# A hybrid retention, mLSTM and feed-forward layer: context keys and values of all heads made first, transposes and scan steps placed later

## The chip, the core and the metric

The kernel runs on one core of a Trainium2 chip. Its engines are TensorE (PE, matrix products; PEld is its weight load), VectorE (DVE), ScalarE (ACT), GpSimd (POOL) and SyncE (SP), whose queue issues nearly all DMA transfers. The metric is the time of one execution on the chip in microseconds (us); the time before is the median of three runs.

## The reference

One layer over 1024 latent tokens of width 1024, with 256 context tokens ahead of them. Two token mixers share one input projection: retention with 4 heads of 128, and mLSTM with 4 heads of 128. Each scans in chunks of 128 tokens in both directions, over the context first, and the latent scan starts from the context's final state. Cut to what matters:

```python
hc = modulate(rms_norm(ctx, norm1_gain), csh1, csc1)      # 256 context tokens
feats_c, post_c = mixer_inputs(hc, w_in, ..., None)       # no rotation
ret_c, ml_c, st_f, st_b = bidirectional_scans(feats_c, log_gamma, zero, zero)
hx = modulate(rms_norm(x, norm1_gain), sh1, sc1)          # 1024 latent tokens
feats_x, post_x = mixer_inputs(hx, w_in, ..., rope)       # q and k of the retention heads rotated
ret_x, ml_x, _, _ = bidirectional_scans(feats_x, log_gamma, st_f, st_b)
x = x + g1 * mixer_output(ret_x, ml_x, *post_x, w_ret_up, w_ml_up, w_out)
x = x + g2 * swiglu(modulate(rms_norm(x, norm2_gain), sh2, sc2), w_ffn_in, w_ffn_out)
return rms_norm(x, final_gain)                            # the context itself is not returned
```

Shift, scale and gate (`sh1`, `sc1`, ...) come from a product of SiLU(c) with the adaLN weights. Of the context only keys, values and mLSTM gates matter, since its outputs are not returned.

## The kernel before

Every fp32 operand of a large product is split into two parts, high and low, and a product is three matmuls: high by high, high by low, low by high. `split` makes the high part on ScalarE (L182) and the low part on VectorE (L183). A weight tile of 128x512 is loaded into `raw` (four buffers) by SP's queue and split into `fw` (eight buffers).

**Start.** The eight tiles of the first half of x are loaded, then the adaLN weights (32 tiles, L396). The context comes later (`load_ctx`), as do the weights of head 0. x and the context are normalized and modulated tile by tile (`scaled_tile`), and head 0's products on the first half of x run between the adaLN products (`first_tiles`, L428 to L430). Head 0 takes its products plainly.

**Heads 1 to 7.** A head has two blocks: one for k and v, one for q and the output gate. A block is a Winograd product of seven products of twelve matmuls of 512 columns (`winograd_block`, `prod`, L251), with left factors that `Factors` makes of four weight tiles and right factors (`t1` to `t4`) that are made once, on VectorE, after head 0. `run_blocks` interleaves the last two products of a block with the first of the next, and after each product calls `tick`, by which the work "beside" advances: the mLSTM gates beside head 1, and from head 2 on the scan of head u - 2, each with a rate in steps per tick:

```python
                if u >= 2:
                    beside(scan(u - 2), 1.3)
```

**Context.** In the k and v block of every head, after its fifth product, `context_kv` computes keys and values of the 256 context tokens: 48 matmuls of 256 columns (L559 to L561) with the head's weights as the stationary operand, four transposes (L568), and a store to `kv_d`. The split context was stored to DRAM (`ctx_d`) and is loaded again for each head in four pairs of tiles (`context_stream`); the right weights need one more factor, `a21`, in these blocks.

**Outputs of a block.** `head_done` gets each quarter. A retention head's k and q are rotated (`rotated`): two DMAs swap the halves, GpSimd and VectorE combine them (L521 to L524). `store_tokens` transposes k, v and the mLSTM gate on TensorE (L509), four transposes a quarter, and stores them.

**Scan.** One step a slot, with each part of a chunk's work in a slot of its own. `load` and `load_qk` bring k, v and q of a chunk (`qk` has two buffers), `decay` scales v on GpSimd (L806), `advance` updates the state (L820), `stage_a` scales q, `stage_b` makes the scores (L866), `stage_c` the output (L883 to L885), `norm_y` normalizes four chunks on VectorE (L910), and `put_y` transposes them (L915):

```python
        for j in range(8):
            after(5 + j, load_qk, j)
            at(6 + j, stage_a, j)
            at(7 + j, stage_b, j)
            at(8 + j, stage_c, j)
        for j0 in (0, 4):
            at(12 + j0, norm_y, j0)
            at(13 + j0, put_y, j0)
```

After the heads come eight blocks for the merge gates (scans 6 and 7 beside the first of them), the up and output projections, the feed-forward part and its output.

The order of instructions on each engine is not the order in which the code writes them: the framework's scheduler places each instruction on its engine, and each engine then works its list in order, waiting where an operand or a buffer is not ready.

Of the kernel before, what the change touches and what calls it, by code (L numbers as in the profile page):

```python
# [17 lines left out]
P = 128  # L18
# [3 lines left out]
KT = 8  # L22
# [12 lines left out]
def body(tc, a, out):  # L35
# [173 lines left out]
    class Factors:  # L209
# [3 lines left out]
        def __init__(self, src, a21=False):  # L213
            self.src, self.a21, self.made = src, a21, []
# [4 lines left out]
        def make(self, r):  # L219
# [13 lines left out]
            if self.a21:  # L233
                yield parts_of(r["a21"])

        def need(self, n=8):
# [32 lines left out]
    def winograd_block(w, x, t, done, new, snaps, tail=None):  # L269
# [35 lines left out]
        if tail is not None:  # L305
            tail()
# [38 lines left out]
    def wt(dt=F32):  # L345
        return pw.tile([P, 512], dt, tag="wt", bufs=5, name=nm("wt"))
# [16 lines left out]
    ctx_d = dram.tile([2, 4, P, 512], F32, name="ctx_d")  # L363
# [9 lines left out]
    def ssq_of(xr, n):  # L373
        ss = [st.tile([P, 512], F32, tag="ss", bufs=2, name=nm("ss"))[:, :n] for _ in range(2)]
        for kt in range(KT):
# [3 lines left out]
            else:  # L379
                sq = st.tile([P, 512], F32, tag="sq", bufs=2, name=nm("sq"))[:, :n]  # L380
# [33 lines left out]
    def plain_pair(w, src, kh):  # L414
        for f in range(2):
            raw = w_raw()
            nc.sync.dma_start(raw, src[kh, f])
            w[("a11", "a21", "a12", "a22")[2 * kh + f]] = parts_of(raw)

    first_ps = [mm_ps(), mm_ps()]  # L420

    def first_tiles(kts):

        for f in range(2):
            for kt in kts:
                wh, wl = (t[:, kt % 4 * P:(kt % 4 + 1) * P] for t in w_kv[("a11", "a21", "a12", "a22")[2 * (kt // 4) + f]])
                hi, lo = xh[0][0][:, kt, :], xh[0][1][:, kt, :]
                nc.tensor.matmul(first_ps[f], lhsT=wh, rhs=hi, start=kt == 0, stop=False, skip_group_check=True)  # L428
                nc.tensor.matmul(first_ps[f], lhsT=wh, rhs=lo, start=False, stop=False, skip_group_check=True)
                nc.tensor.matmul(first_ps[f], lhsT=wl, rhs=hi, start=False, stop=kt == KT - 1, skip_group_check=True)  # L430

    load_x(x_raw[0], a["xT"][0])
# [14 lines left out]

    def scaled_x(hf, kt):
# [3 lines left out]
        (0, 3): lambda: cols_of("x0", x_raw[0], 512),  # L452
        (2, 5): lambda: cols_of("c", c_raw, CTX),
        (3, 5): lambda: cols_of("x1", x_raw[1], 512),
    }
    loads = {
        9: lambda: plain_pair(w_kv, a["win"][0], 0),
        14: lambda: plain_pair(w_kv, a["win"][0], 1),
        19: load_ctx,
        25: lambda: load_x(x_raw[1], a["xT"][1]),  # L460
        36: lambda: plain_pair(w_qg, a["win"][1], 0),
        38: lambda: plain_pair(w_qg, a["win"][1], 1),
    }
    for cb in range(4):
        ada_ps[cb] = sc_ps()[:2, :]
        for kt in range(KT):
# [27 lines left out]
    kv_d = [dram.tile([P, NCH, 2, P], F32, name=f"kv_d{u}") for u in range(2 * H)]  # L494
# [10 lines left out]
    def store_tokens(c, dst):  # L505

        pt_ = sc_ps()
# [6 lines left out]
    def head_done(u, part):  # L514
        def rotated(c, hf, scale):
# [4 lines left out]
            o = wt()  # L520
# [9 lines left out]
        def done(f, hf, c):  # L530
            n0 = slice(2 + 4 * hf, 6 + 4 * hf)
            t = slice(hf * 512, hf * 512 + 512)
            if part == 0 and f == 0:
                o = rotated(c, hf, None) if u < H else c
                nc.sync.dma_start(qk_d[u][:, 1, t], o)
                store_tokens(o, kv_d[u][:, n0, 0, :])
            elif part == 0:
                store_tokens(c, kv_d[u][:, n0, 1, :])
# [8 lines left out]
            else:  # L547
                store_tokens(c, g_d[u][:, 4 * hf:4 * hf + 4, :])
        return done

    def context_kv(u, w, parts):

        pk, pv = sc_ps(), sc_ps()
        for kt in range(KT):
            hi, lo = parts(kt)
            for f, ps in enumerate((pk, pv)):
                wh, wl = (t[:, kt % 4 * P:(kt % 4 + 1) * P] for t in w(2 * (kt // 4) + f))
                o = ps[:, :CTX]
                nc.tensor.matmul(o, lhsT=wh, rhs=hi, start=kt == 0, stop=False)  # L559
                nc.tensor.matmul(o, lhsT=wh, rhs=lo, start=False, stop=False)  # L560
                nc.tensor.matmul(o, lhsT=wl, rhs=hi, start=False, stop=kt == KT - 1)  # L561
        c = wt()
        nc.scalar.copy(c[:, :CTX], pk[:, :CTX])
        nc.scalar.copy(c[:, CTX:], pv[:, :CTX])
        pt_ = sc_ps()
        for n in range(2):
            for f in range(2):
                nc.tensor.transpose(pt_[:, (2 * n + f) * P:(2 * n + f + 1) * P], c[:, f * CTX + n * P:f * CTX + (n + 1) * P], ident)  # L568
        o = wt()
        nc.scalar.copy(o, pt_)  # L570
        nc.sync.dma_start(kv_d[u][:, 0:2], o.rearrange("p (n f c) -> p n f c", n=2, f=2))

    def context_stream():

        last = {}

        def parts(kt):
            if kt % 2 == 0:
                for i in range(2):
                    last[i] = wt(F32R)  # L580
                    nc.sync.dma_start(last[i].bitcast(F32), ctx_d[i, kt // 2])
# [811 lines left out]
```

## Time and profile before

| | us |
|---|---|
| median of three runs (lowest, highest) | 1719.94 (1718.01, 1721.85) |
| the profiled execution | 1724.97 |
| its span in the trace | 1723.2 |
| TensorE busy | 1607.6 (93%) |
| VectorE busy | 1008.2 (59%) |
| ScalarE busy | 690.9 (40%) |
| GpSimd busy | 434.2 (25%) |

The stages in the span: start and head 0 to 126.7 us, head 1 to 211.9, heads 2 to 7 to 656.1, the first merge gates with the last scans to 770, the other gates and projections to 1075, the feed-forward products to 1460, their output to the end. In a row of a table by stage stand the stretch, its length, and then the busy time of PE, PEld, DVE, ACT and POOL with the number of instructions; behind them the granted clock of TensorE as a share of full speed, the share of the DMA engines, and GB/s. A wait stands with the instruction that waited, what released it, the total, the count and the longest.

### The profile page before, as it was taken

To read this page: it belongs to the slowest core of one execution; us is meant where nothing else is said; L and a number is where in the kernel's file an instruction comes from. 1 tells how busy PE (TensorE), PEld (TensorE's weight loads), DVE (VectorE), ACT (ScalarE), POOL (GpSimd) and SP (SyncE) were. 2 spreads that over 40 slices of the span, in tenths; PEclk is the share of its full clock that TensorE was granted. 3 is DMA by queue.
4 is the path that set the end of the run, shared out by engine and by line. 5 is a ranking of instruction groups with operands and counts; after the bars stand their busy time and mean duration, and the time that the engine had idled before them with its cause. 6 is when DMAs were issued, how large, how long until landed. Compare 5 with 4: busy or idle time off the path is not lost.

```text
span 1723.2 us, 23184 instructions
## 1 busy us (share of the span) xinstructions
PE 1607.6 (93%) x7702; PEld 1300.6 (75%) x7702; DVE 1008.2 (59%) x1986; ACT 690.9 (40%) x1355; POOL 434.2 (25%) x504
## 2 busy tenths in 40 slices
PE   7987788888998989999999999999999999999997
PEld 2665667777777777878888887788888888888887
DVE  4568757575575757766444579555554454636343
ACT  4433333333343436665422345334444334524230
POOL 1251134343233434421022026322222221000001
PEclk9998889999999999999999999999999999999998
DMA  9433376676767766645645440432222223845531
GB/s 319 151 107 103 111 241 209 215 232 196 235 202 220 225 203 192 193 128 176 216 139 185 157 142 6 134 93 85 90 88 80 74 85 118 276 120 154 195 92 50
DMA packets 188632, 268.64 MB, mean 156 GB/s; under 512 B 19504, under 2 KB 82992, under 8 KB 188512
## 3 DMA queue, kind: packets, MB, share of 16 engines
q1 hardware_dynamic: 186640, 265.06, 49.6%
q10 hardware_dynamic: 1872, 2.10, 0.4%
q8 instruction: 61, 1.00, 0.2%
q14 instruction: 59, 0.48, 0.1%
HBM read 204.42 MB, written 58.47 MB: 153 GB/s over the span
## 4 chain that ended last, share of the span: by engine, by line
PE 59%; DVE 13%; DMA 12%; issue 4%; POOL 3%; ACT 3%; SPq 1%; DVEq 0%; POOLq 0%; ACTq 0%
PE ch L251 15%; PE ts L251 13%; DMA qk<-qk_d 3%; DMA wt<-ctx_d 3%; PE ch L1253 2%; PE ch L1254 2%; PE ch L1252 2%; PE ts L1252 2%; PE ts L1254 2%; PE ts L1253 2%; DMA raw<-wffn 2%; DVE fw L183 2%; DMA kv<-kv_d 2%; PE ch L104 1%; PE ch L103 1%
## 5 line engine op out<-in xcount | busy, mean ns | idle before, releaser
L251 PE MATMUL ts<-A,fw 128*128 128x512 f32 x1176 | 300.8, 400 | 6.4 <-ACT A L386 2.3
L183 DVE TENSOR_TENSOR fw<-raw,fw 128x512 fp32r<-128x512 f32 x282 | 198.3, 707 | 179.5 <-ACT fw L182 179.1
L251 PE MATMUL ch<-A,fw 128*128 128x512 f32 x1176 | 296.6, 395 | 0.0
L251 PEld LDWEIGHTS ts<-A,fw 128*128 128x128 f32 x1176 | 221.2, 192 | 61.2 <-DVE A L388 4.6
L251 PE MATMUL ch<-t,fw 128*128 128x512 f32 x1008 | 256.9, 399 | 8.1 <-ACT u L286 3.4
L182 ACT CAST fw<-raw 128x512 fp32r<-128x512 f32 x282 | 172.4, 621 | 206.3 <-PE ch L1254 86.5
L251 PEld LDWEIGHTS ch<-A,fw 128*128 128x128 f32 x1176 | 220.2, 189 | 45.1 <-ACT wt L286 0.9
L251 PEld LDWEIGHTS ch<-t,fw 128*128 128x128 f32 x1008 | 188.9, 191 | 48.9 <-ACT t L182 4.6
L183 DVE TENSOR_TENSOR fw<-stg,fw 128x512 fp32r<-128x512 f32 x126 | 96.6, 767 | 85.3 <-ACT fw L182 85.0
L1122 POOL TENSOR_TENSOR hid<-hid,sg 128x512 f32<-128x512 f32 x44 | 86.8, 1974 | 236.7 <-ACT fw L182 158.4
L251 PE MATMUL ts<-t,fw 128*128 128x512 f32 x504 | 136.4, 405 | 7.1 <-ACT t L182 6.0
L182 ACT CAST fw<-stg 128x512 fp32r<-128x512 f32 x126 | 78.3, 622 | 137.0 <-DVE stg L221 58.0
L251 PEld LDWEIGHTS ts<-t,fw 128*128 128x128 f32 x504 | 94.4, 191 | 28.0 <-ACT t L182 8.0
L286 ACT COPY u<-ch 128x512 f32<-128x512 f32 x104 | 60.9, 585 | 135.9 <-PE ch L251 134.3
L221 POOL TENSOR_TENSOR stg<-raw,raw 128x512 f32<-128x512 f32 x42 | 61.4, 1462 | 147.7 <-DVE fw L183 83.7
L806 POOL TENSOR_SCALAR vs<-kv,dcol 128x128 f32<-128x128 f32 x72 | 54.3, 761 | 123.8 <-PE sc L820 53.0
L806 POOL TENSOR_SCALAR vs<-kv,colq 128x129 f32<-128x129 f32 x72 | 56.9, 794 | 101.2 <-PE sc L820 80.9
L954 DVE SCALAR_TENSOR_TENSOR acc<-stg,silu_c,acc 128x256 f32<-128x256 f32 x112 | 60.2, 538 | 19.2 <-DMA stg<-wada 17.9
L1244 POOL TENSOR_SCALAR cp<-cp,cpack 128x256 f32<-128x256 f32 (+1 forms) x6 | 8.2, 1363 | 223.1 <-ACT stg L1298 223.1
L820 PE MATMUL sc<-vs,kv 128*128 128x128 f32 (+1 forms) x288 | 52.6, 286 | 7.9 <-POOL vs L806 4.8
L820 PEld LDWEIGHTS sc<-vs,kv 128*128 128x128 f32 x288 | 44.6, 194 | 13.9 <-POOL vs L806 6.9
L221 DVE TENSOR_TENSOR stg<-raw,raw 128x512 f32<-128x512 f32 x42 | 40.0, 952 | 22.5 <-DMA raw<-wffn 15.6
(371 smaller groups left out, 3002.0 us busy)
## 6 DMA issues: line engine op xcount, KB each, us to landing
raw<-wffn SPq DMA_DIRECT2D x88, 256.0 KB
raw<-wfo SPq DMA_DIRECT2D x88, 256.0 KB
kv<-kv_d SPq DMA_DIRECT2D x152, 128.0 KB
raw<-win SPq DMA_DIRECT2D x64, 256.0 KB
stg<-wada SPq DMA_DIRECT2D x64, 256.0 KB
wt<-ctx_d SPq DMA_DIRECT2D x56, 256.0 KB
hid_d<-hid SPq DMA_DIRECT2D x44, 256.0 KB
kv_d<-wt SPq DMA_DIRECT2D x40, 256.0 KB
```

Source lines behind the costliest of these rows:

```text
L182: nc.scalar.copy(hi, x)
L183: nc.vector.tensor_tensor(out=lo, in0=x, in1=hi.bitcast(F32), op=ALU.subtract)
L221: eng.tensor_tensor(out=o, in0=x, in1=y, op=op)
L251: nc.tensor.matmul(ps, lhsT=w[wp_][:, c], rhs=x[xp][k], start=start and k == i == 0, stop=cont or (stop and k == 3 and i == 2), skip_group ...
L286: nc.scalar.copy(o, chain)
L806: nc.gpsimd.tensor_scalar(out=vs, in0=kv[d, n][1], scalar1=col, scalar2=None, op0=ALU.mult)
L820: nc.tensor.matmul(ps, lhsT=kv[d, n][0], rhs=vsd.pop((d, n)), start=True, stop=True)
L954: nc.vector.scalar_tensor_tensor(out=acc, in0=r2, scalar=s, in1=acc, op0=ALU.mult, op1=ALU.add)
L1122: nc.gpsimd.tensor_tensor(out=c, in0=c, in1=sgs[f, hf], op=ALU.mult)
L1252: nc.tensor.matmul(ps, lhsT=w[0][:, c], rhs=h[0][:, t], start=kt == 0, stop=False)
L1253: nc.tensor.matmul(ps, lhsT=w[0][:, c], rhs=h[1][:, t], start=False, stop=False)
L1254: nc.tensor.matmul(ps, lhsT=w[1][:, c], rhs=h[0][:, t], start=False, stop=kt == 2 * NG - 1)
```

## The change

It has four parts.

1. **Context first.** A new input `wctx` holds k and v weights of two heads side by side, 512 columns, in four pairs. The context is loaded before everything else and scaled between the adaLN products; `ctx_tiles` then makes keys and values with 128 context tokens as the stationary operand and the 512 weight columns moving, so that the result has tokens on the partitions and is stored without a transpose. Pairs 0 and 1 run between the adaLN products, 2 and 3 before head 0. `context_kv`, `context_stream`, `ctx_d` and the factor `a21` are gone, and so is `first_tiles`: head 0 runs all its products behind the context. x is loaded after the adaLN weights.
2. **Transposes later.** `store_tokens` puts its transposes on a list, with 2 ticks for k and 1 for others; `tick` runs them.
3. **Scan.** Decays, states, scores and outputs have one or two slots more behind their loads, `qk` three buffers; `put_y` stands two slots behind `norm_y` where it was one. The rate is 1.55 steps a tick where it was 1.3. The decay tables are made per head.
4. **Memory.** `fw` has seven buffers for eight, `wt` four for five; the heads' outputs have four buffers of their own (`kt`).

```diff
-        t = wp.tile([P, 2, 512], F32R, tag="fw", bufs=8, name=nm("fw"))
+        t = wp.tile([P, 2, 512], F32R, tag="fw", bufs=7, name=nm("fw"))
...
-            if self.a21:
-                yield parts_of(r["a21"])
...
-        if tail is not None:
-            tail()
...
-        return pw.tile([P, 512], dt, tag="wt", bufs=5, name=nm("wt"))
+        return pw.tile([P, 512], dt, tag="wt", bufs=4, name=nm("wt"))
...
+    def ctx_tiles(pair, kts):
+        for kt in kts:
+            wh, wl = ctx_w.pop((pair, kt))
+            for n in range(2):
+                if kt == 0:
+                    ctx_ps[pair, n] = mm_ps()
+                ps = ctx_ps[pair, n]
+                hi, lo = (t[kt][:, n * P:(n + 1) * P] for t in ch)
+                nc.tensor.matmul(ps, lhsT=hi, rhs=wh, start=kt == 0, stop=False)
+                nc.tensor.matmul(ps, lhsT=hi, rhs=wl, start=False, stop=False)
+                nc.tensor.matmul(ps, lhsT=lo, rhs=wh, start=False, stop=kt == KT - 1)
+                if kt == KT - 1:
+                    c = wt()
+                    nc.scalar.copy(c, ps)
+                    for i in range(2):
+                        nc.sync.dma_start(kv_d[2 * pair + i][:, n].rearrange("p f c -> p (f c)"), c[:, i * CTX:(i + 1) * CTX])
...
-    load_x(x_raw[0], a["xT"][0])
+    load_ctx()
...
+            for k_ in (2 * cb - 2, 2 * cb - 1):
+                for pair in range(2):
+                    ctx_tiles(pair, (k_,))
+                    ctx_load()
...
+    for kt in range(KT):
+        ctx_tiles(2, (kt,))
+        ctx_load()
+        scaled_x(0, kt)
...
+    def store_tokens(c, dst, ticks):
+        pending.append([ticks, lambda: transpose_out(c, dst)])
+
+    def run_pending(all_=False):
+        for p in list(pending):
+            p[0] -= 1
+            if p[0] <= 0 or all_:
+                pending.remove(p)
+                p[1]()
...
-            at(i // 2 + 1, decay, 1, n)
-            at(i // 2 + 2, advance, 1, n)
+            at(i // 2 + 2, decay, 1, n)
+            at(i // 2 + 3, advance, 1, n)
...
-            qk[j] = bt([P, 2, P], "qk", 2)
+            qk[j] = bt([P, 2, P], "qk", 3)
...
-            after(5 + j, load_qk, j)
+            after(6 + j, load_qk, j)
...
-            at(6 + j, stage_a, j)
-            at(7 + j, stage_b, j)
-            at(8 + j, stage_c, j)
+            at(8 + j, stage_a, j)
+            at(9 + j, stage_b, j)
+            at(10 + j, stage_c, j)
...
-            at(12 + j0, norm_y, j0)
-            at(13 + j0, put_y, j0)
+            at(14 + j0, norm_y, j0)
+            at(16 + j0, put_y, j0)
...
-                    beside(scan(u - 2), 1.3)
+                    beside(scan(u - 2), 1.55)
```

In the changed kernel the lines have moved: L249 is the product of a block (L251 before), L441 to L443 the context's products, L554 the token transposes (L509), L824 the state update (L820), L870 the scores (L866), L887 to L889 the output (L883 to L885).

Three places on TensorE follow, in its scheduled order. First the start, behind the second column block of adaLN (L396): before, the products of the first half of x with head 0's weights (`A` holds x, `fw` the weights).

```order
L396 MATMUL sc_268<-araw_263,silu_c 2x512
L396 MATMUL sc_268<-araw_266,silu_c 2x512
L428 MATMUL ts_149<-A_116,fw_182 128x512
L429 MATMUL ts_149<-A_117,fw_182 128x512
L430 MATMUL ts_149<-A_116,fw_182 128x512
```

Now the same place holds the context's products (`t` and `clo` are the context's two parts):

```order
L395 MATMUL sc_265<-araw_263,silu_c 2x512
L441 MATMUL ts_323<-fw_183,t_140 128x512
L442 MATMUL ts_323<-fw_183,t_140 128x512
L443 MATMUL ts_323<-fw_183,clo_144 128x512
L441 MATMUL ch_327<-fw_183,t_140 128x512
L442 MATMUL ch_327<-fw_183,t_140 128x512
L443 MATMUL ch_327<-fw_183,clo_144 128x512
```

The first of the two names behind the arrow moves or stands as the text says: x moved with its 512 columns, and now the weights move while 128 context tokens stand still; two accumulators take turns with each weight tile.

Second, head 4's k and v block with the scan of head 2 beside it. Before, behind the context's loop (its last transposes are L568; L958 belongs to the second adaLN product), these steps stand together:

```order
L820 MATMUL sc_3694<-vs_3580,kv_3508 128x128
L568 MATMUL sc_3681<-cpack,wt_3678 128x128 x3
L866 MATMUL sc_3699<-qk_3543 128x128
L820 MATMUL sc_3710<-vs_3697,kv_3538 128x128
L883 MATMUL sc_3715<-sf_3693,qs_3582 128x128
L884 MATMUL sc_3715<-sb_3369,qs_3582 128x128
L866 MATMUL sc_3723<-qk_3586 128x128
L885 MATMUL sc_3715<-kv_3538,W_3701 128x128
L820 MATMUL sc_3775<-vs_3713,kv_3584 128x128
L883 MATMUL sc_3780<-sf_3709,qs_3703 128x128
L884 MATMUL sc_3780<-sb_3369,qs_3703 128x128
```

Now, in the same block, a step stands ahead of a product:

```order
L824 MATMUL sc_3826<-vs_3787,kv_3714 128x128
L887 MATMUL sc_3831<-sf_3783,qs_3777 128x128
L888 MATMUL sc_3831<-sb_3456,qs_3777 128x128
L889 MATMUL sc_3831<-kv_3714,W_3798 128x128
L870 MATMUL sc_3838<-qk_3716 128x128
L249 MATMUL ch_3421<-A_118,fw_3540 128x512
L249 MATMUL ch_3421<-A_119,fw_3540 128x512
L249 MATMUL ch_3421<-A_118,fw_3540 128x512 x2
```

Before, two state updates, two scores and two outputs follow each other with no product between them; now the step ends with its score, and the twelve matmuls of a product follow, of which the first three rows are shown; further on in the block two steps stand together.

Third, the transposes of a rotated k of head 2, the first of its two. Before, they stand behind the first product of the next block (`ch_2174`), whose last matmuls are shown, and two state updates stand behind them:

```order
L251 MATMUL ch_2174<-A_116,fw_2153 128x512 x2
L251 MATMUL ch_2174<-A_117,fw_2153 128x512
L251 MATMUL ch_2174<-A_116,fw_2153 128x512
L509 MATMUL sc_1980<-cpack,wt_1975 128x128 x4
L820 MATMUL sc_1993<-vs_1946,kv_1918 128x128
L820 MATMUL sc_1997<-vs_1948,kv_1906 128x128
L251 MATMUL ts_2378<-t_1085,fw_2158 128x512
```

Now they stand ten matmuls into the last product of their own block (`ch_1961`):

```order
L249 MATMUL ch_1961<-A_118,fw_2080 128x512 x2
L249 MATMUL ch_1961<-A_119,fw_2080 128x512
L249 MATMUL ch_1961<-A_118,fw_2080 128x512 x2
L554 MATMUL sc_2230<-cpack,kt_2183 128x128 x4
L554 MATMUL sc_2238<-cpack,kt_2228 128x128 x4
L824 MATMUL sc_2251<-vs_2206,kv_2158 128x128
```

The transposes have moved from the next block's first product into their own block's last, and those of v stand right behind them.

## Rows read from the trace of the kernel before

**Rows 1.** Windows by stage: busy us of each engine, granted clock, DMA share, GB/s
```profile
...
0.00:126.70 126.70, 107.72 (x451) 65.64 (x452) 67.99 (x159) 52.34 (x92) 37.60 (x43) 0.99 0.56 190
126.70:211.90 85.20, 63.02 (x268) 47.51 (x267) 67.41 (x102) 33.00 (x69) 10.42 (x9) 0.80 0.39 114
211.90:656.10 444.20, 392.29 (x2190) 326.51 (x2189) 284.63 (x717) 169.41 (x415) 160.89 (x243) 0.98 0.71 215
656.10:770.00 113.90, 108.71 (x589) 92.05 (x588) 80.70 (x229) 72.96 (x162) 50.00 (x98) 0.99 0.57 168
...
1075.00:1460.00 385.00, 381.03 (x1662) 311.90 (x1661) 200.40 (x261) 152.04 (x264) 94.31 (x61) 1.00 0.30 91
```

**Rows 2.** The page's chain that ended last, by line
```profile
...
PE ch L251 15%; PE ts L251 13%; DMA qk<-qk_d 3%; DMA wt<-ctx_d 3%; PE ch L1253 2%; PE ch L1254 2%; PE ch L1252 2%; PE ts L1252 2%; PE ts L1254 2%; PE ts L1253 2%; DMA raw<-wffn 2%; DVE fw L183 2%; DMA kv<-kv_d 2%; PE ch L104 1%; PE ch L103 1%
```

**Rows 3.** TensorE's waits, 211.9 to 770: us in total, times, longest
```profile
...
PE sc L915 <- DVE o L910: 11.2, 11, 2.6
PE sc L509 <- DVE wt L524: 8.2, 4, 5.4
PE sc L866 <- DMA qk<-qk_d: 7.8, 10, 1.7
PE sc L559 <- DMA wt<-ctx_d: 7.1, 5, 2.0
PE sc L509 <- DVE wt L281: 5.9, 6, 1.6
PE sc L820 <- POOL vs L806: 4.8, 5, 2.1
PE sc L560 <- DMA wt<-ctx_d: 3.7, 7, 1.2
```

**Rows 4.** TensorE's longest wait, 126.7 to 211.9
```profile
...
PE sc L568 <- ACT wt L564: 7.0, 1, 7.0
```

**Rows 5.** TensorE's longest wait, 0 to 126.7
```profile
...
PE sc L396 <- DMA araw<-wada: 12.3, 1, 12.3
```

**Rows 6.** Timeline of TensorE: start, us, instruction, count [idle before]
```profile
...
84.11 0.28 PE L559 MATMUL sc<-t,fw 128*128 128x256 f32 x1
...
85.17 0.28 PE L559 MATMUL sc<-t,fw 128*128 128x256 f32 x1
...
115.02 2.88 PE L251 MATMUL ch<-A,fw 128*128 128x512 f32 x12
117.74 2.88 PE L251 MATMUL ts<-A,fw 128*128 128x512 f32 x12
```

**Rows 7.** Timeline of TensorE, head 2: after the third sum's product, and the transposes
```profile
...
224.22 2.88 PE L251 MATMUL ch<-t,fw 128*128 128x512 f32 x12
...
236.72 1.11 PE L509 MATMUL sc<-cpack,wt 128*128 128x128 f32 x4 [5.44 <-DVE wt L524]
```

**Rows 8.** The chain: start, us, what; head 3, then a burst of scan steps
```profile
...
302.19 0.71 PE ts L251 x3
...
311.36 0.66 PE sc L509 x4
...
405.10 4.24 DMA qk<-qk_d
```

**Rows 9.** The page's groups for one split: busy, mean ns, idle before
```profile
...
L183 DVE TENSOR_TENSOR fw<-raw,fw 128x512 fp32r<-128x512 f32 x282 | 198.3, 707 | 179.5 <-ACT fw L182 179.1
...
L182 ACT CAST fw<-raw 128x512 fp32r<-128x512 f32 x282 | 172.4, 621 | 206.3 <-PE ch L1254 86.5
```

**Rows 10.** Windows, 20 to 40 us
```profile
...
20.00:40.00 20.00, 20.00 (x64) 6.89 (x65) 11.28 (x32) 6.57 (x14) 2.30 (x2) 1.00 0.95 325
```

**Rows 11.** Timeline of VectorE: first right-hand factor, and the instruction after the last
```profile
...
130.64 0.69 DVE L651 TENSOR_TENSOR wt<-t,t 128x512 f32<-128x512 f32 x1
...
155.44 0.68 DVE L281 TENSOR_TENSOR wt<-ts,u 128x512 f32<-128x512 f32 x1
```

**Rows 12.** SP queue's waits for a split, 211.9 to 770
```profile
...
SPq L202 <- DVE fw L183: 12.2, 15, 1.9
```

More of the change, by code (lines that the diff above doesn't have):

```diff
@@ L362, in body @@
     ch = [[t[k // 2][:, (k % 2) * CTX:(k % 2 + 1) * CTX] for k in range(KT)] for t in (chi, clo)]
-    ctx_d = dram.tile([2, 4, P, 512], F32, name="ctx_d")
+    kv_d = [dram.tile([P, NCH, 2, P], F32, name=f"kv_d{u}") for u in range(2 * H)]
     def load_x(dst, src):
@@ L417, in plain_pair, with ctx_load @@
             nc.sync.dma_start(raw, src[kh, f])
[L418 to L430, printed above, removed]
-    load_x(x_raw[0], a["xT"][0])
+            hi, lo = w_parts() if last is None or f == 0 else last
+            split(hi, lo, raw)
+            w[("a11", "a21", "a12", "a22")[2 * kh + f]] = hi, lo
+    ctx_ps, ctx_w = {}, {}
+    ctx_order = [(p, k) for k in range(KT) for p in range(2)] + [(p, k) for p in (2, 3) for k in range(KT)]
+    def ctx_load(n=1):
+        for _ in range(n):
+            if ctx_order:
+                pair, kt = ctx_order.pop(0)
+                raw = w_raw()
+                nc.sync.dma_start(raw, a["wctx"][pair, kt])
+                ctx_w[pair, kt] = parts_of(raw)
+    def ctx_tiles(pair, kts):
[15 more added lines that the diff above has]
+    load_ctx()
     raws = {(0, kt): ada_load(0, kt) for kt in range(KT)}
@@ L547, in done @@
             else:
-                store_tokens(c, g_d[u][:, 4 * hf:4 * hf + 4, :])
+                store_tokens(c, g_d[u][:, 4 * hf:4 * hf + 4, :], 1)
         return done
[L551 to L581, printed above, removed]
-            c = slice(kt % 2 * CTX, (kt % 2 + 1) * CTX)
-            return last[0][:, c], last[1][:, c]
-        return parts
     QK = ("a11", "a21", "a12", "a22")
     done_kv, done_qg = head_done(0, 0), head_done(0, 1)
-    for f in range(2):
-        c = wt()
-        nc.scalar.copy(c, first_ps[f])
-        done_kv(f, 0, c)
-    for k in range(KT):
-        scaled_tile("c", c_raw, ch[0][k], ch[1][k], k, 1)
-        if k % 2:
-            nc.sync.dma_start(ctx_d[0, k // 2], chi[k // 2].bitcast(F32))
-            nc.sync.dma_start(ctx_d[1, k // 2], clo[k // 2].bitcast(F32))
     wgt = [st.tile([P, 4, P], F32R, tag="araw", bufs=10, name=nm("wgt")) for _ in range(2)]
@@ L616, in gate_products @@
         nc.sync.dma_start(e_d[:, t0:t0 + n], e)
[L618 to L629 removed]
+    gate_products(0, CTX, lambda i, kt: ch[i][kt])
+    gate_products(CTX, 512, lambda i, kt: xh[0][i][:, kt, :])
+    for w, done in ((w_kv, done_kv), (w_qg, done_qg)):
+        for f in range(2):
+            ps = mm_ps()
+            prod(ps, w[QK[f]], quad(xh[0], 0), True, False)
+            prod(ps, w[QK[2 + f]], quad(xh[0], 4), False, True)
+            run_pending()
+            c = head_tile()
+            nc.scalar.copy(c, ps)
+            done(f, 0, c)
+            scaled_x(1, 4 * (w is w_qg) + 2 * f)
+            scaled_x(1, 4 * (w is w_qg) + 2 * f + 1)
     ps4 = {}
@@ L780, in scan @@
         slots, ends = {}, {}
-        dec, dcol, dt_all, g128, mask = (held[k] for k in ("dec", "dcol", "dt", "g128", "mask"))
+        g128, mask = held["g128"], held["mask"]
+        if ret:
+            dt_, dec, dcol = decay_tables(h)
         def at(slot, fn, *args):
@@ L991, in head @@
         def head(u, part):
[L992 removed]
+            w = Factors(a["win"][2 * u + part])
             def first():
@@ L1014, in first @@
                 if blk in (0, 2):
-                    beside(scan(2 * H - 2 + blk // 2), 1.3)
+                    beside(scan(2 * H - 2 + blk // 2), 1.55)
                 if blk == 5:
@@ L1207, in w2_tiles @@
             nc.sync.dma_start(raw, a["wfo"][dp, b])
-            hi, lo = sub(extra, 2 + b - 8) if extra is not None and b >= 8 else w_parts()
+            hi, lo = sub(extra, b - 5) if extra is not None and b >= 7 else w_parts()
             split(hi, lo, raw)
```

125 lines of the change are left out of this document (60 added, 65 removed).

## The prediction

> **What bounds the kernel now.** I read the busy time by stretches first [rows 1], then the chain by line [rows 2], then TensorE's waits stretch by stretch [rows 3 to 5], and last single instructions for their prices [rows 6 to 11]. The reader is to see three things. First, TensorE sets the time: in the feed-forward part (1075 to 1460) it is busy 381.0 of 385 us, so nothing done outside TensorE can shorten that part [rows 1]. Second, the stretch in which heads 2 to 7 run with the scans beside them (211.9 to 656.1) has room: 444.2 - 392.3 = 51.9 us idle, and 5.2 more from 656.1 to 770, 57.1 in all; before that, 22.2 us are idle in head 1 (126.7 to 211.9, where the granted clock is 0.80) and 19.0 in the first 126.7 [rows 1]. Third, what ends these waits: the chain holds 3% each of loads of `ctx_d` and of `qk_d`, some 50 us each [rows 2], while as waits of TensorE they come to 7.1 + 3.7 and 7.8 us, beside 8.2 + 5.9 at the token transposes (L509), 11.2 at the output transposes (L915) and 4.8 at the state update (L820) [rows 3]. The chain counts a whole transfer, the waits only what TensorE stood still; I price by the waits.
>
> **Prices.** Twelve products of 512 columns take 117.74 - 115.02 = 2.72 us, 0.227 each; nine of 256 columns 85.17 - 84.11 = 1.06 us, 0.118 each [rows 6]; four transposes 0.66 us [rows 8]. Splitting a weight tile costs 0.62 us of ScalarE and 0.71 of VectorE [rows 9].
>
> **Start, 0 to 126.7.** Added on TensorE: 4 pairs x 8 tiles x 2 chunks x 3 = 192 products of 512 columns, 43.6 us. Removed: head 0's context, 48 x 0.118 = 5.7 us, and its four transposes, 0.7. That is +37.2, and almost none of it fills a hole: from 20 to 40 us TensorE is busy all 20 us although the DMA engines move 325 GB/s there [rows 10]. The first wait, 12.3 us for the first adaLN weight [rows 5], gets shorter, since 1 MB of context stands ahead of it where 2 MB of x stood: 1 MB at 325 GB/s is 3.2 us. Of the other 19.0 - 12.3 = 6.7 us idle I take 6 off, as products whose data is long there now stand between the steps that waited. Splits: 32 more, 22.6 us of VectorE and 19.9 of ScalarE, where VectorE is busy 68.0 of 126.7 us [rows 1]; the 43.6 us of products cover them. That cover is thin in one place: between the last adaLN product and the first of x, VectorE must do some 16 splits, two sums of squares, eight scaled tiles of x and head 0's splits, about 40 us, beside some 30 of TensorE. Uncovered, that adds about 8 us (a bound; the other end is 0, which I take because a third of it can be done earlier). Loads: 8 MB more at 325 GB/s are 26 us, under 37.2 us of products. On SP's queue x now stands behind 16 tiles of context weights, but its scaling is needed only after pairs 2 and 3, 22 us later. Sum: 37.2 - 3.2 - 6 = +28 us.
>
> **Head 1, 126.7 to 211.9.** Its context goes, 5.7 + 0.7, and the wait of 7.0 at its transposes [rows 4]: 13.4. VectorE makes the right-hand factors of x without a gap from 130.64 to 155.44 [rows 11], after the last rotated q of head 0, and TensorE waits for them; that order stays, so this wait does. The gates' steps stay on VectorE too (67.4 of 85.2 busy), and the 7.0 ended with a ScalarE copy that stood behind them, so part will come back elsewhere: I take -8. The clock I leave at 0.80; at 0.99 its 63.0 busy us would be some 51, which stands in the best rival alone.
>
> **Heads 2 to 7 with the scans, 211.9 to 770.** Six contexts, 6 x (5.7 + 0.7) = 38.2 us of TensorE. Their waits for `ctx_d`: 10.8.
>
> Token transposes wait 14.1 us. One or two products later in the program is not that in the scheduled order. Summing the rows' prices between the last product of a rotated k and its transposes, I get 5.8 and 15.8 us for head 2's two, 6.7 and 14.9 for head 3's; after the change 13.0, 11.1, 7.1 and 6.4. A rotation (two swaps through SP's queue, GpSimd, VectorE) took 302.90 to 311.36 = 8.5 us once, and 224.2 to 236.7 = 12.5 where the wait of 5.44 stood [rows 7, 8]. The 5.44 goes (13.0); by 8.5 us the others leave 1.4 + 2.1, by 12.5 us 1.4 + 5.4 + 6.1. So the 8.2 falls by 4.7 or grows by 4.7. I take 0; bounds -14.1 and +13.
>
> Output transposes: the order puts only some 1.5 us more between the VectorE step and them; 6 of 11.2. For `qk_d` the chain says most: in one burst a load takes 4.24 us [rows 8], because with two buffers it can only be issued when the scores two chunks back are done, and with no product between them the steps follow each other in about 1 us (the order above). Now one or two steps stand between twelve products, and a third buffer lets the load start a step sooner; from the score that frees a buffer to the one that needs it I count 7 to 10 us of TensorE, where it was 3 to 4. So 7 of 7.8 at L866, and 3 of 4.8 at L820. Sum: 38.2 + 10.8 + 6 + 7 + 3 = -65 us.
>
> By the Trainium skill, page "DMA: Bandwidth & Descriptors", section "Anatomy of one DMA — SWDGE (gpsimd) path", a transfer costs about 2.0 us plus its bytes at 436 GB/s, for 128 KB an estimate of 2.3. These loads go by SP's queue, for which that section gives no fit; if it held there, 3 to 4 us would cover a load, the waits at L866 would not be the loads', and the sum would be 7 us less. The trace has 4.24, and the rows' price is the one I keep.
>
> Does another engine take the place? VectorE has 284.6 us in 444.2; six splits fewer are -4, and in some 385 us that is a share of 73%. The nearest row is 656.1 to 770: VectorE 80.7 of 113.9 (71%), scans and products and no context, and TensorE idle 5.2 of 113.9, 5% [rows 1]. What I leave idle is 57.1 - 26.8 = 30.3 of 493, 6%. Nothing is added back.
>
> **The rest.** Seven buffers for split weights instead of eight: a factor waits one product (2.72 us) longer for its buffer. In the feed-forward part it is needed six products after it is made, so 0; the upper bound is the slow rival. Smaller pools (four `wt`) lie where TensorE doesn't wait for them: 0.
>
> **Sum.** +28 - 8 - 65 = -45. The profiled execution took 1724.97 us (span 1723.2), 5.0 over the median of the three runs: 1724.97 - 45 - 5.0 = 1675.
>
> **Rivals.**
> *The start costs more and half the scan waits stay*: VectorE's 40 us are not covered (+8), the 6 don't come back, head 1 gives only its 6, the scans 8 of 16: 42 - 6 - 38.2 - 10.8 - 8 = -21, 1699 us. For it: VectorE alone sits between a loaded weight and its product. Against: weights are loaded up to eleven tiles ahead. Chance 0.17.
> *The waits merely move*: the program's scheduler, not the slot, sets the order, and the slow rotation holds: 28 - 8 - 38.2 - 10.8 + 5 = -24, 1696 us. For it: the distances above grew in one place of four. Against: those at L866 do grow. Chance 0.12.
> *Everything comes off*: the start hides better (+24), head 1 gives 16, and of the 57.1 idle 45 go: 24 - 16 - 38.2 - 45 = -75, 1645 us. For it: idle is 1% in the feed-forward part. Against: VectorE's 73%. Chance 0.14.
> *Slower: the missing buffer blocks the load queue.* With seven, the splits of a block's last two factors wait for products 5 and 6 of the block before; until they are made, the next block's raw loads wait on SP's queue, and every load of a scan stands behind them. SP already waits 12.2 us, 15 times, for such a split [rows 12]. If each of the 16 blocks passes 2.72 us on (+43.5), no scan wait goes, and the start costs 42 with head 1 at -6: 43.5 + 42 - 6 - 49 = +30, 1750 us. It decides from about a third of that delay on top of the dear start, and no scan wait gone. Against: the next raw loads are needed four products later. Chance 0.06.
>
> **How the numbers follow.** Forecast 0.49, the rivals as above, 0.02 for cancelling to nothing. The range reaches from the case in which everything comes off to past both dear ones: 1644 to 1704, some 0.8 of the chance. 0.2% (3.4 us) is about what a measurement of this kernel can tell from no change: faster 0.91, same 0.03, slower 0.06.
>
> **What would show it.** TensorE's rows for the context: 192 of 512 columns, all before about 100 us, no wait on `ctx_d`. Head 1's products begin near 155 us, head 2's near 232; from there to where the scans end some 493 us instead of 558, TensorE idle about 30. L866 gone from the top of the waits, L554 (the token transposes) not. Wrong, if head 1 begins after 170, if TensorE waits for split weights in the start, or if SP's wait for splits grows among the heads.

## The result and the profile after

The changed kernel takes 1672.49 us (median of four runs, 1671.8 to 1677.89), the kernel before 1719.62 beside it (1718.01 to 1721.85): a ratio of 0.9732, with a 95% interval of 0.9709 to 0.9755. Forecast were 1675 us and a range of 1644 to 1704. The profiled executions stand 1724.97 - 1672.67 = 52.3 us apart (spans 1723.2 and 1670.9), against a forecast of 45 between them; the medians are 47.1 apart. The profiled execution before lies 5.4 us above its median, the one after 0.2, so some 5 us of the differences by stage below belong to that one execution.

The windows of the changed kernel, cut where the same work begins as in [rows 1] (columns: PE, PEld, DVE, ACT, POOL, granted clock, DMA share, GB/s):

```profile
0.00:156.60 156.60, 144.08 (x590) 96.86 (x591) 89.87 (x196) 75.70 (x130) 37.94 (x38) 0.99 0.65 212
156.60:209.70 53.10, 45.36 (x185) 33.69 (x184) 45.52 (x75) 23.67 (x42) 11.97 (x14) 0.94 0.40 112
209.70:599.90 390.20, 352.19 (x1907) 292.25 (x1906) 304.46 (x734) 172.93 (x417) 170.72 (x243) 0.97 0.71 213
599.90:715.80 115.90, 107.94 (x589) 90.54 (x589) 85.76 (x233) 71.26 (x162) 49.88 (x98) 1.00 0.56 172
...
1022.80:1407.70 384.90, 381.55 (x1676) 315.30 (x1675) 205.98 (x266) 150.95 (x264) 99.62 (x61) 1.00 0.29 91
```

Stage by stage, from the lengths of these rows and of [rows 1]:

| stage | before | after | difference | forecast |
|---|---|---|---|---|
| start and head 0 | 126.7 | 156.6 | +29.9 | +28 |
| head 1 | 85.2 | 53.1 | -32.1 | -8 |
| heads 2 to 7 and four gate blocks | 558.1 | 506.1 | -52.0 | -65 |
| the rest of the span | 953.2 | 955.1 | +1.9 | 0 |

Two later profiles of the changed kernel, `changed_beside` and `changed_again`, have these stages to within 1.1 us.

The sum is near; two of its terms are not. Head 1 gave 24 us more than I took, the heads after it 13 less. The feed-forward part is the same as before to 0.1 us.

TensorE's waits from 209.7 to 715.8, to be read against [rows 3] (the lines have moved: L919 answers to L915, L554 to L509, L824 to L820, L962 to L958):

```profile
PE sc L919 <- DVE o L914: 9.0, 6, 1.8
PE sc L554 <- DVE kt L279: 7.4, 6, 2.9
PE sc L740 <- issue: 5.6, 1, 5.6
PE sc L962 <- DVE acc L958: 4.6, 4, 2.6
PE sc L824 <- POOL vs L810: 3.7, 1, 3.7
PE sc L554 <- DVE kt L569: 3.5, 4, 1.4
PE sc L895 <- DVE W L875: 3.5, 9, 1.1
PE sc L824 <- issue: 2.1, 2, 1.8
```

The loads are gone from the list: neither `ctx_d` (10.8 us before) nor `qk_d` (7.8) stands there. What took their place are mostly waits for VectorE: L740, the transposes of the mLSTM gates, which stood in head 1 before (the list gives it no releaser; it is followed to VectorE further down), L962 (4.6, where L958 had 1.4 before), and L895.

### The profile page after: what moved, and what is told of

It reads as the page before. It is cut to its first block, busy times and chain, and to the rows that moved or that the text cites. A ratio compares the mean times of both kernels' runs of the same rounds, so it can differ in the third digit from the quotient of the medians.

```text
span 1670.9 us, 22762 instructions
## 1 busy us (share of the span) xinstructions
PE 1583.0 (95%) x7478; PEld 1283.3 (77%) x7478; DVE 1034.6 (62%) x2011; ACT 704.3 (42%) x1368; POOL 448.0 (27%) x504
## 4 chain that ended last, share of the span: by engine, by line
PE 65%; DVE 12%; DMA 7%; POOL 4%; issue 4%; ACT 2%; SPq 1%; DVEq 0%; POOLq 0%; ACTq 0%
PE ch L249 20%; PE ts L249 16%; DMA stg<-wada 3%; PE ch L1255 2%; PE ch L1254 2%; PE ch L1253 2%; PE ts L1253 2%; PE ts L1255 2%; PE ts L1254 2%; DVE acc L958 2%; DVE fw L183 2%; POOL hid L1123 1%; PE ts L104 1%; PE ch L104 1%; PE ts L103 1%
## 5 line engine op out<-in xcount | busy, mean ns | idle before, releaser
L183 DVE TENSOR_TENSOR fw<-raw,fw 128x512 fp32r<-128x512 f32 x305 | 222.6, 735 | 145.9 <-ACT fw L182 145.1
L249 PE MATMUL ts<-A,fw 128*128 128x512 f32 x1200 | 298.0, 394 | 3.6 <-DVE wt L279 1.8
L249 PE MATMUL ch<-A,fw 128*128 128x512 f32 x1176 | 294.0, 397 | 1.9 <-ACT wt L284 1.9
L182 ACT CAST fw<-raw 128x512 fp32r<-128x512 f32 x305 | 187.9, 621 | 246.4 <-PE ch L1255 86.6
L249 PEld LDWEIGHTS ts<-A,fw 128*128 128x128 f32 x1200 | 222.5, 188 | 51.8 <-DVE A L387 3.0
L249 PE MATMUL ch<-t,fw 128*128 128x512 f32 x1008 | 254.8, 400 | 6.1 <-ACT u L284 3.7
L249 PEld LDWEIGHTS ch<-A,fw 128*128 128x128 f32 x1176 | 221.4, 191 | 48.8 <-ACT wt L284 2.9
L249 PEld LDWEIGHTS ch<-t,fw 128*128 128x128 f32 x1008 | 190.0, 191 | 47.6 <-ACT u L284 5.1
L1123 POOL TENSOR_TENSOR hid<-hid,sg 128x512 f32<-128x512 f32 x44 | 90.3, 2064 | 217.1 <-DVE hid L279 201.3
L249 PE MATMUL ts<-t,fw 128*128 128x512 f32 x504 | 128.9, 397 | 4.2 <-ACT t L182 3.2
L249 PEld LDWEIGHTS ts<-t,fw 128*128 128x128 f32 x504 | 93.4, 189 | 24.6 <-ACT t L182 4.2
L810 POOL TENSOR_SCALAR vs<-kv,dcol 128x128 f32<-128x128 f32 x72 | 60.0, 840 | 63.6 <-DMA kv<-kv_d 37.1
L958 DVE SCALAR_TENSOR_TENSOR acc<-stg,silu_c,acc 128x256 f32<-128x256 f32 x112 | 61.3, 547 | 17.7 <-DMA stg<-wada 16.8
L824 PE MATMUL sc<-vs,kv 128*128 128x128 f32 (+1 forms) x288 | 53.9, 296 | 7.0 <-POOL vs L810 3.7
L183 DVE TENSOR_TENSOR fw<-s,fw 128x512 fp32r<-128x512 f32 x42 | 31.1, 740 | 46.5 <-ACT fw L182 46.4
L824 PEld LDWEIGHTS sc<-vs,kv 128*128 128x128 f32 x288 | 45.7, 200 | 13.9 <-POOL vs L810 6.8
```

Of the source, the lines that this page charges most:

```text
L182: nc.scalar.copy(hi, x)
L183: nc.vector.tensor_tensor(out=lo, in0=x, in1=hi.bitcast(F32), op=ALU.subtract)
L249: nc.tensor.matmul(ps, lhsT=w[wp_][:, c], rhs=x[xp][k], start=start and k == i == 0, stop=cont or (stop and k == 3 and i == 2), skip_group ...
L810: nc.gpsimd.tensor_scalar(out=vs, in0=kv[d, n][1], scalar1=col, scalar2=None, op0=ALU.mult)
L824: nc.tensor.matmul(ps, lhsT=kv[d, n][0], rhs=vsd.pop((d, n)), start=True, stop=True)
L958: nc.vector.scalar_tensor_tensor(out=acc, in0=r2, scalar=s, in1=acc, op0=ALU.mult, op1=ALU.add)
```

## The experiments

Ratios are to the kernel before, measured beside each. `no_later_context`, `scan_back`, `scan_only` and `transposes_at_once` ran on one chip, `qk_two`, `transposes_later_still` and `gate_rate` on a second, `scan_back_beside`, `ada_first` and `no_gate_scans` on a third, some ten minutes apart. The changed kernel itself ran beside the second and the third group, with 0.9752 (0.9729 to 0.9775) and 0.9700 (0.9684 to 0.9715). So a difference of 0.005 between groups says nothing, and kernels are compared within a group where that is possible. Nor do a few us in one stage of one profile: the work behind the gate blocks, which none of these edits touches, took from 951.3 us (`scan_back_beside`) to 960.8 (`ada_first`).

**The context alone (`no_later_context`).** The kernel before, with the contexts of heads 1 to 7 left out.

```diff
-        nc.sync.dma_start(kv_d[u][:, 0:2], o.rearrange("p (n f c) -> p n f c", n=2, f=2))
+        for v in range(2 * H):
+            nc.sync.dma_start(kv_d[v][:, 0:2], o.rearrange("p (n f c) -> p n f c", n=2, f=2))
...
-                                                    kv_tail(u, w) if part == 0 else None)
+                                                    None)
```

> The kernel before, with the context keys and values of heads 1 to 7 left out: head 0's are stored in their place, and the factor a21 goes. The start stays as it was. By my prediction's terms this saves 38.2 + 10.8 in heads 2 to 7 and 6.4 + 7.0 less a part that comes back (8 in all) in head 1: 57 us, 1663. By what the trace after shows, head 1 saves far more, since its waits and with them the clock change: some 25 there and 49 later, 74 in all, 1646. A rival: the context's products gave the scans time, and without them the loads of a scan are waited for: under 45 us, over 1675.

Measured: 1662.34 us beside 1723.32, ratio 0.9648 (0.9621 to 0.9675), 61 us. That is near my 57, and not the 74 of the second reading. Its windows for head 1, heads 2 to 7 and the gate blocks:

```profile
122.30:189.50 67.20, 51.52 (x189) 36.87 (x188) 61.05 (x88) 25.92 (x47) 9.62 (x9) 0.82 0.34 95
189.50:589.50 400.00, 350.82 (x1905) 290.05 (x1904) 289.31 (x723) 164.50 (x409) 161.26 (x244) 0.97 0.67 205
589.50:704.40 114.90, 108.71 (x589) 91.88 (x588) 79.87 (x229) 73.09 (x162) 50.64 (x98) 0.99 0.55 167
```

Head 1 takes 67.2 us for 85.2, heads 2 to 7 400.0 for 444.2: 18.0 and 44.2, where my terms were 8 and 49. The total is near them partly by luck: the start, where nothing goes, is 4.4 us shorter (122.3 for 126.7), and the work behind the gate blocks 4.6 longer. In heads 2 to 7 TensorE's work fell by 392.3 - 350.8 = 41.5 us and its idle time only from 51.9 to 49.2. The reader is to see what became of the waits for `ctx_d`: the longest are now the token transposes of rotated k and the output transposes, 13.5 and 13.9 us, where they were 8.2 and 11.2 [rows 3].

```profile
PE sc L916 <- DVE o L911: 13.9, 9, 2.7
PE sc L509 <- DVE wt L524: 13.5, 3, 9.1
PE sc L509 <- DVE wt L281: 8.0, 8, 2.1
...
PE sc L867 <- DMA qk<-qk_d: 5.1, 5, 2.0
```

In head 1 the 7.0 us at L568 did not go either; TensorE waits 5.7 us at a token transpose instead:

```profile
PE sc L509 <- DVE wt L524: 5.7, 1, 5.7
```

The VectorE step that ends it (L524) runs from 178.19 us, between the gates' scans, which begin at 169.72.

So waits of TensorE that went were replaced by a VectorE result that was late next, and the qk waits fell only from 7.8 to 5.1 us. With the start's +29.9 us, the context part is worth 61 - 30 = 31 us; by my terms it was -28 + 57 = 29.

**The scan part (`scan_back`, `scan_back_beside`).** The changed kernel with it undone, run twice.

```diff
...
-            qk[j] = bt([P, 2, P], "qk", 3)
+            qk[j] = bt([P, 2, P], "qk", 2)
...
-            at(8 + j, stage_a, j)
-            at(9 + j, stage_b, j)
-            at(10 + j, stage_c, j)
+            at(6 + j, stage_a, j)
+            at(7 + j, stage_b, j)
+            at(8 + j, stage_c, j)
...
-                    beside(scan(u - 2), 1.55)
+                    beside(scan(u - 2), 1.3)
...
```

> The changed kernel with the scan part undone: the slots and the rate of 1.3 as before, two qk buffers. My prediction gave this part 7 + 6 + 3 = 16 us, so by it the time is about 1672 + 16 = 1688 us, and the waits for qk loads at the scores (7.8 us in the kernel before) come back. The rival: these waits only change their name, as the transposes' and the gates' did, and the time stays within 4 us of 1672. A third: with the context loop gone, the old slots are enough, since the steps no longer crowd behind it; then the qk waits stay near zero too.

> The changed kernel with the scan part undone, now beside the changed kernel itself. My prediction's term of 16 us has fallen already; what is open is whether the part is worth about 9 us, as the spans of the two profiled executions say (1680.0 and 1670.9), or 0 to 4, as the ratios measured in different hours say. 9 us would be 0.980 of the kernel before here; 0 to 4, 0.974 to 0.977.

Measured: 1680.95 us, ratio 0.9753 (0.9739 to 0.9768), and beside the changed kernel 1679.78 against 1671.63, 0.9751 (0.9738 to 0.9764) against 0.9700 (0.9684 to 0.9715). The part is worth 0.0051 of the time before, 8.8 us (some 5 to 12 by the two intervals), about half of the 16 I gave it. The decay tables made per head were not undone with it, and slots and rate were not taken apart. Of the second run and then the changed kernel beside it, the heads from 2 to 7, the gate blocks, and the next block:

```profile
208.90:610.20 401.30, 354.36 (x1907) 291.97 (x1906) 308.43 (x733) 172.51 (x416) 166.55 (x243) 0.97 0.69 207
610.20:723.30 113.10, 107.45 (x589) 90.75 (x589) 79.40 (x228) 72.27 (x161) 49.48 (x98) 1.00 0.55 170
723.30:742.40 19.10, 19.10 (x86) 15.78 (x85) 13.00 (x20) 12.91 (x24) 1.32 (x1) 1.00 0.74 235
```

```profile
209.00:599.40 390.40, 352.14 (x1907) 292.14 (x1906) 304.09 (x734) 172.96 (x417) 167.89 (x243) 0.97 0.71 213
599.40:715.00 115.60, 107.80 (x590) 90.46 (x590) 86.50 (x233) 71.24 (x162) 48.82 (x98) 1.00 0.57 173
715.00:736.20 21.20, 19.33 (x86) 15.66 (x85) 14.54 (x22) 13.27 (x24) 2.75 (x2) 1.00 0.61 198
```

In these two profiles, which stand only 3.8 us apart (spans 1674.6 and 1670.8), the part takes 10.9 us out of the heads and gives 2.5 back in the gate blocks and 2.1 in the block after them. The longest waits of the kernel with it undone (`scan_back_beside`) are these:

```profile
PE sc L919 <- DVE o L914: 10.7, 10, 3.0
PE sc L824 <- POOL vs L810: 7.6, 7, 3.3
...
PE sc L870 <- DMA qk<-qk_d: 4.0, 5, 2.1
```

With the context first and the old slots, the loads of qk were waited for 4.0 us, and 5.6 in `scan_back`, not 7.8: part of what I booked for the slots had gone with the context loop already.

**One buffer more (`qk_two`).** The changed kernel with two qk buffers.

```diff
-            qk[j] = bt([P, 2, P], "qk", 3)
+            qk[j] = bt([P, 2, P], "qk", 2)
```

> The changed kernel with two qk buffers. With the whole scan part undone the loads of qk were waited for 5.6 us at the scores, and 0 in the changed kernel. If the third buffer is what took them away, as my prediction said first, they come back here, about 5 us of wait and 3 to 6 us of time. If the longer distance between a load and its scores does it, no such wait, and within 2 us of the changed kernel.

Measured: 1676.02 us beside the changed kernel's 1676.61, 0.9754 and 0.9752. The wait comes back with 1.8 us, and no time can be seen:

```profile
PE sc L870 <- DMA qk<-qk_d: 1.8, 3, 1.4
```

Of the 4.0 to 5.6 us that stand with the old slots, the greater distance between a load and its scores, with the new rate, takes 2.2 to 3.8, the buffer 1.8.

**The scan part in the old kernel (`scan_only`).** The kernel before with the new slots and the new rate, and two qk buffers.

> The kernel before with the scan part alone: the new slots and 1.55 steps a tick, but two qk buffers as before, since three find no room. By my prediction's terms, without the buffer's share of the 7 us, about -9 to -12 us: 1709. The rival, that the crowding behind the context loop sets these waits and not the slots: within 4 us of 1720.

Measured: 1728.58 us, 1.0031 (1.0017 to 1.0045): 5 us slower. Neither reading had that; the rival's is nearer. The rows are heads 2 to 7 and the gate blocks, which took 444.2 and 113.9 before, and two of its waits there:

```profile
211.30:652.70 441.40, 396.27 (x2190) 327.80 (x2189) 288.08 (x719) 170.30 (x416) 165.51 (x243) 0.97 0.71 217
652.70:772.30 119.60, 109.16 (x590) 91.93 (x589) 83.76 (x232) 70.72 (x162) 49.20 (x98) 0.99 0.56 168
```

```profile
PE sc L915 <- DVE o L910: 13.5, 8, 3.1
...
PE sc L866 <- DMA qk<-qk_d: 3.6, 6, 1.8
```

The gate blocks got longer and the heads little shorter: the waits for qk are half of the 7.8 us, but those at the output transposes grew from 11.2. The new slots and rate paid in the changed kernel and not here. That the context loop makes this difference, by pushing the steps together, is argued and not shown.

**The transposes (`transposes_at_once`, `transposes_later_still`).** The changed kernel with the token transposes issued at once, and with all of them one tick later than in the change.

```diff
-        pending.append([ticks, lambda: transpose_out(c, dst)])
+        transpose_out(c, dst)
```

> The changed kernel with the token transposes issued where store_tokens stands, as before; nothing else changes. My prediction took 0 us for this part, between -14.1 and +13: by it 1672 within 3 us. If later transposes do save their old waits, this costs up to 14 us (1686); if they stand too early in the order, undoing gains up to 8 (1664).

> The changed kernel with every token transpose a tick later again (3 for k, 2 for the others). Placing them at once cost some 12 us although the waits at the transposes themselves were the same. If lateness is worth time by itself, this gives some more, 3 to 8 us below the changed kernel. If what counted is how the scheduler's order of the scans and gates around them fell out (head 2's first block alone was 11 us longer with the transposes at once), this can go either way: within 8 us, and the difference stands in one or two blocks, not in all.

Measured: 1689.33 us, 0.9797 (0.978 to 0.9813), for the first; 1677.02, 0.9761 (0.9739 to 0.9784), for the second, beside the changed kernel's 0.9752. The changed kernel did not run beside the first. Against its three ratios (0.9700 to 0.9752) the part is worth 8 to 17 us, where I took 0. But it isn't lateness as such: a tick more gives nothing. And it is hardly the wait at the transposes: in the kernel with the transposes at once, from 211.1 to 731.9, they have 12.1 us, in the changed one 11.5 (7.4 and 3.5 above, and 0.6 for a third kind). What grew is the wait of the state update (L824) for GpSimd's scaled v, 10.5 where the changed kernel has 3.7:

```profile
PE sc L824 <- POOL vs L810: 10.5, 6, 5.4
...
PE sc L962 <- DVE acc L958: 7.5, 6, 1.9
PE sc L740 <- issue: 6.5, 1, 6.5
PE sc L554 <- DVE kt L279: 5.5, 6, 1.9
PE sc L554 <- DVE kt L569: 5.3, 3, 2.4
...
PE sc L554 <- ACT kt L277: 1.3, 2, 0.6
```

Of the 18.7 us between the two profiles (spans 1689.6 and 1670.9; the first is the slowest of its four executions) 11.3 stand in one place, head 2's k and v block: with the transposes at once 51.4 us at a clock of 0.83 (first row), in the changed kernel 40.1 at 0.79 (second).

```profile
211.10:262.50 51.40, 33.68 (x169) 27.19 (x168) 38.12 (x59) 17.03 (x38) 19.62 (x20) 0.83 0.48 141
```

```profile
209.70:249.80 40.10, 30.54 (x140) 24.18 (x139) 30.45 (x47) 12.07 (x28) 11.34 (x14) 0.79 0.49 143
```

The rows hold 169 and 140 TensorE instructions: 33.68 - 30.54 = 3.1 us are work that the scheduler put into this block, the rest is waiting, most of it at the state update, which has 3.7 us in the changed kernel's block and here:

```profile
PE sc L824 <- POOL vs L810: 8.5, 3, 5.4
```

Why the edit orders that block so, the runs don't show.

**Gate scans (`no_gate_scans`).** The changed kernel without the six VectorE scans of the mLSTM gates.

```diff
-                nc.vector.tensor_tensor_scan(out=v(bb), data0=v(rm), data1=v(gf), ...)
-                nc.vector.tensor_tensor_scan(out=v(m), data0=v(gf), data1=v(gi), ...)
+                pass
```

> The changed kernel with the six VectorE scans of the mLSTM gates left out (cumulated gates and running maximum stay zero). They hold VectorE for 11.2 us while TensorE waits 5.6 us at the gate transposes (L740) and 3.7 at the state update behind them; in the kernel before they stood behind the 7.0 us at L568. If they are what this wait comes from in both kernels, it goes here and head 2 begins earlier or has a first block shorter: 6 to 12 us of time. If VectorE's other work is as late without them, under 4 us.

Measured: 1672.36 us beside 1671.63, 0.9698 and 0.9700: no difference. The wait at the gate transposes is gone, and head 2's second block begins at 242.4 us instead of 249.8; but the gain of 7.4 us there is 6.1 by the gate blocks (593.8 for 599.9), 4.3 at their end (711.5 for 715.8) and 2.9 in the span (1668.0 for 1670.9), and the medians show nothing of it. The theory named the right wait and gave it the wrong price. Its gate blocks had a lower clock, 0.97, than the changed kernel's 1.00 and took 117.7 us for 115.9.

**The first load (`ada_first`) and the gate blocks' rate (`gate_rate`).**

```diff
-    load_ctx()
-    raws = {(0, kt): ada_load(0, kt) for kt in range(KT)}
+    raws = {(0, kt): ada_load(0, kt) for kt in range(4)}
+    load_ctx()
+    raws.update({(0, kt): ada_load(0, kt) for kt in range(4, KT)})
```

> The changed kernel with the first four adaLN tiles loaded ahead of the context. TensorE's first wait is 8.5 us for the first adaLN tile, behind 1 MB of context. If that wait sets the start, it falls by some 2 to 3 us (1 MB at the 294 GB/s of the first slice of the changed kernel's profile is 3.6) and the time with it. If the context's own chain (square sums, scaling) sets the end of the start, nothing within 2 us.

> The changed kernel with the scans of heads 6 and 7, beside the merge gates, at 1.75 steps a tick instead of 1.55. With the scan part undone the four gate blocks and the next took 5 us less than in the changed kernel, as a scan has 21 slots now and 19 before, and ends later. If the end of these scans is late, 1.75 gives 2 to 5 us; if VectorE sets the pace there (71 to 74% busy), within 2 us.

Measured: 1676.75 us, 0.9727 (0.9714 to 0.974), for the first, above the changed kernel's 0.9700 beside it; 1675.0, 0.9738 (0.9718 to 0.9759), for the second, the same as the changed kernel's 0.9752. With the adaLN tiles first, TensorE's first wait fell from 8.5 to 6.1 us and changed its releaser:

```profile
PE sc L395 <- ACT silu_c L354: 6.1, 1, 6.1
PE sc L141 <- DVE ss L381: 1.4, 2, 1.2
```

Now ScalarE's SiLU of c ends it, and the context's square sums are waited for; the start ends at 155.6 for 156.6 us. Why the whole is some 5 us slower is open: where the gate blocks end, its profile is 2.9 us ahead (712.9 for 715.8), and at its end 2.9 behind (spans 1673.8 and 1670.9), so it falls behind where nothing was changed.

No kernel of these that does the whole work beats the changed one. The parts measured here, 31 for the context, 8.8 for the scans and 8 to 17 for the transposes, come to 48 to 57 us beside the whole's 47 to 52. The memory part (one `fw` and one `wt` buffer fewer, `kt` apart) was not run by itself; the sums leave little for it, but no run shows that it costs nothing.

## Why the prediction was right

**The start (+28, measured +29.9).** Its large terms held. TensorE is busy 144.1 of 156.6 us there, 36.4 more than before where 192 products less the old context are 37.2; the first wait fell from 12.3 to 8.5 us, by 3.8 where I took 3.2. The third term was too large: of the other 6.7 us idle I took 6 off, and 12.5 - 8.5 = 4.0 are left, so 2.7 went. The splits of the context weights were covered: waits for a split in the start come to 2.0 us in all, 1.8 of them at the context's products.

```profile
PE sc L395 <- DMA araw<-wada: 8.5, 1, 8.5
PE ts L442 <- DVE fw L183: 1.8, 2, 1.0
```

**Head 1 (-8, measured -32.1).** This step failed. I wrote that the wait for the right-hand factors stays, that part of the 7.0 us comes back elsewhere, and that the clock stays at 0.80. The factors' wait did stay, with 6.3 us of 10.6; its longest rows before and after:

```profile
PE ts L251 <- ACT t L182: 6.0, 4, 2.5
```

```profile
PE ts L249 <- ACT t L182: 3.2, 2, 1.7
```

(VectorE did not make them quite without a gap before: one of 1.19 us stands at 133.25, ahead of the last step of a rotation.) The 7.0 was a ScalarE copy behind the gates' chain on VectorE, as I said, and it did come back: VectorE's gate scans end at 219.1 us, and the transposes of their result (L740) wait for the subtraction behind them, which ends at 221.08.

```profile
207.88 2.81 DVE L705 TENSOR_TENSOR_SCAN g<-g,g 4x1280 f32<-4x1280 f32 x1
...
219.60 1.48 DVE L715 TENSOR_TENSOR g<-g,g 36x1280 f32<-36x1280 f32 x1
```

```profile
221.18 0.50 PE L740 MATMUL sc<-cpack,g 36*128 36x36 f32 x3 [5.64 <-issue]
```

But they stand in head 2 now, so head 1 shows all the gain and head 2 the price. Of head 1's 32.1 us, 22.2 - 7.7 = 14.5 are idle time and 63.0 - 45.4 = 17.6 busy time. Of these 17.6, the context's products and transposes are 6.4, and the gate transposes, which took 3.4 us there (201.35 to 204.70), have moved; the remaining 8 are nearly all the clock, 0.94 instead of 0.80: the head's own products take 7.2 us less (rows in the last section). I had left that to the best rival. It rose in two places. At the factors TensorE had 0.83 and 0.60 before (130 to 145 and 145 to 160 us), and now, with less waiting there,

```profile
156.00:171.00 15.00, 12.65 (x52) 9.10 (x50) 12.60 (x19) 7.45 (x13) 3.63 (x6) 1.00 0.42 110
171.00:186.00 15.00, 10.54 (x29) 6.33 (x29) 13.90 (x21) 7.01 (x13) 4.01 (x4) 0.77 0.10 21
```

And behind the wait at L568 it had 0.81 and 0.73 (175 to 190 and 190 to 205 us); that wait and its low clock, 0.79 in head 2's first block, are in the next stage now. The context's leaving alone brings neither: in `no_later_context` head 1 has 0.82 in all and 0.51 at the factors (137 to 152 us), and the wait behind the gates' chain stays in it. How much of each stage's miss the boundary alone makes, no run tells; the two stages together came to -84.1 where I had -73.

**Heads 2 to 7 (-65, measured -52.0).** The work held, the waits did not: of the 52.0 us 40.9 are work that went, where I had 38.2, and 11.1 idle time, where I had 26.8. TensorE's work fell by 40.1 us in the stretch up to the gate blocks (392.3 to 352.2), although 2.2 us of gate transposes came in, and the 10.8 us of `ctx_d` are gone. The moved gate transposes bring 5.6 us of wait beside their own time. The scan part was mis-sized, 16 us for a measured 8.8: the output transposes lost 2.2 us and not 6 (11.2 to 9.0), the state update's wait for GpSimd 1.1 and not 3 (4.8 to 3.7), and only L866 went as forecast, 2.2 to 3.8 us of it with the context loop, 4.0 to 5.6 with the slots, the rate and the third buffer. The token transposes were mis-sized the other way, 0 for a measured 8 to 17, though not where I looked: at L554 itself 2.6 us went (14.1 to 11.5).

**The sum.** The mechanism held in its main term: the context's work moved into 36.4 us of products ahead, and its work and waits behind them went. That the sum came out so near was in part luck: two misses in the parts, some 7 us too much for the scans and some 8 to 17 too little for the transposes, cancelled. The check of what TensorE would be left idle let too much pass: I had 30.3 us from head 2 to the last scan, and the windows show 38.0 + 8.0 = 46. VectorE, to which I gave a share of 73% there, has 304.5 of 390.2 us, 78%, with the gates' chain now in this stretch. So "nothing is added back" was wrong, by some 16 us. The sign that head 2 begins near 232 us failed too; it begins at 209.7. The slow rival's condition didn't come about: SP's queue waits less for a split from 209.7 to 715.8 than it did before (12.2 us, [rows 12]):

```profile
SPq L202 <- DVE fw L183: 4.6, 5, 1.8
```

## What to carry to other kernels

Price the work that goes from the trace and trust it; price the waits that go with a reserve, since here the context's loads, once gone, left waits for VectorE's results behind, and of the 5.6 us at the gate transposes nothing was left in the time when they went. A wait behind a slow chain on another engine, as at L568, moved to the next instruction that needed the engine, in one run within the stage and in one into the next, with the low clock beside it; so book it over both stages. And an edit that delays emission in a scheduled program must be tried rather than argued: its effect here came mostly from waits that it doesn't name.

## What was not expected of the hardware

The same products of head 1 took 51.3 busy us at a granted clock of 0.80 and 44.2 at 0.94 (the first two rows, of the products' line alone, before and after; the columns are PE and PEld); the row for 145 to 160 us before shows 0.60, the mean of stretches at the two levels, in the midst of TensorE's waits for the factors. And the same kernel, measured three times, had ratios of 0.9700, 0.9732 and 0.9752 to the kernel before: what is smaller than 0.005 had to be measured beside the changed kernel on one chip or not at all.

```profile
126.70:211.90 85.20, 51.33 (x170) 35.91 (x169) 0.80 0.39 114
```

```profile
156.60:209.70 53.10, 44.16 (x169) 31.99 (x168) 0.94 0.40 112
```

```profile
145.00:160.00 15.00, 11.48 (x28) 7.08 (x29) 13.05 (x22) 6.65 (x13) 2.09 (x4) 0.60 0.15 36
```
